# Two layers of a hybrid decoder trunk: the framework's scheduler orders the kernel on another machine model

## Chip, cores and metric

One core of one Trainium2 chip runs the whole kernel. The metric is the device time of one execution in microseconds (us); for the kernel before it is the median of three runs. Engines go by the names of the profile: PE (TensorE matmul), PEld (its weight loads), DVE (VectorE), ACT (ScalarE), POOL (GpSimd), SP (SyncE, which here issues most DMAs).

## The reference, cut to what matters

512 tokens of width 1024 go through two layers. A layer adds three things to x, one after the other: a mixer of three parallel branches, a cross attention over 256 memory tokens, and a gated MLP with a short causal convolution.

```
h = rmsnorm(x)
ya = nsa_attention(...)        # 8 heads: compressed, selected and window attention
yb = hgrn2_recurrence(...)     # gated linear recurrence, 4 heads
yc = gated_deltanet(...)       # delta rule recurrence, 4 heads, triangular solves
merged = sigmoid(h@ma)*(ya@w_branch_a) + sigmoid(h@mb)*(yb@w_branch_b) + sigmoid(h@mc)*(yc@w_branch_c)
x = x + merged @ w_mix_out
x = x + memory_cross_attention(rmsnorm(x), mem_k, mem_v, w_q, q_norm, k_norm, w_o)
x = x + conv_glu_ffn(rmsnorm(x), w_up, conv_w, w_down)     # D_FF = 2816
```

All weights are float32. The three recurrences and attentions of the mixer do not depend on each other; the mixer, the cross attention and the MLP depend on each other in that order, and so do the two layers.

## The kernel before, in words

`tile_trunk` (L200) holds the program. Activations stand as eight tiles of 128 features x 512 tokens. Every dense projection (`dense`, `fm_proj`, `fm_scaled`) goes through `load_w` (L340): SP loads 256 KB of weights into a `wr` buffer (three of them), ACT rounds them to `wh`, DVE subtracts to get the rest `wl` (two buffers of each), and `mm3` issues three matmuls of 128x512 for every 128 rows of weights (high x high, high x low, low x high). One load feeds four times three matmuls. These dense matmuls accumulate in the three `pd` banks. The small matmuls of the recurrences and attentions use two `pa` banks and three `pt` banks; between two of them lie a DVE step, an ACT step, or both.

The order of the program text in a layer is: token projections, delta rule (`gdn`, L518 on: preparation, inverse, levels, a scan over four chunks), HGRN recurrence (`hgrn`, seven levels, then a scan) woven with the preparation of the sparse attention (`nsa_pre`), gates and queries, the attention (`nsa_attn`, 16 steps of one head pair and one block of 128 queries), the three branch projections, the output projection, cross attention (`xattn`, `xo_resid`), MLP (`ffn`). All of this is unrolled.

What sets the order on the engines is not the text but the scheduler of the framework, which works when the `TileContext` closes. Each instruction has a priority from its place in the text. The scheduler plays the program on a machine model: an engine that can take an instruction is given the one of highest priority among those whose inputs and buffers are there in the model's time. The order that results on each engine is written into the program, and the chip runs each engine's list in that order, waiting on semaphores where an input is late. Two kinds of instructions are pulled ahead in priority by 3000 places:

```
with tc.high_priority(PRI):
    act(hi, raw)
    tt(lo, raw, hi.bitcast(F32), SUB)
```

(L345 to L347, the split of the weights) and the scaling that empties a `pd` bank (`fm_scaled`, L446). The numbers of buffers bound how far dense work can run ahead: 16 `gate` tiles hold finished projections, 36 `chain` tiles hold everything of the recurrences and attentions, two `pa` and three `pt` banks hold their products. The helpers `mm` (L236), `act` (L243), `tt` (L246), `ts` (L250, L252) and `stt` (L255) record every operation, so most rows of the profile carry one of these lines.

## Time and profile before

| | us |
|---|---|
| median of 3 runs | 2110.07 |
| lowest, highest | 2108.05, 2112.93 |
| the profiled execution, span from first to last instruction | 2108.7 |
| PE busy in it | 2057.5 |
| DVE busy | 1430.0 |
| ACT busy | 951.3 |
| POOL busy | 131.9 |

The profile lists the span of the profiled execution and no separate time around it; the span lies 1.4 us under the median. Busy time is the time in which at least one instruction of an engine runs. Matmuls overlap each other, so the mean of one is longer than the distance between two.

### The profile page before, as it was taken

The numbers are of one execution on the slowest core, as the hardware profiler recorded it, in microseconds if no ns is written. First come the engines' busy times: TensorE is split into PE (matmuls) and PEld (weight loads), VectorE is DVE, ScalarE is ACT, GpSimd is POOL, SyncE is SP. The second block draws the span as 40 slices with busy tenths as digits, with TensorE's granted clock in tenths as the row PEclk, the third lists the DMA queues.
The fourth block names the chain that finished last, engine by engine and source line by source line (L and its number), as shares of the span: only waits on it lengthen the run. The fifth ranks groups of instructions, "written<-read, shape, count | busy, mean of one in ns | idle before, by whom it ended". The sixth has DMA issues, their size and how long they took to land. (4 is left out here: it accounts for less than half of the span.)

```text
span 2108.7 us, 31046 instructions
## 1 busy us (share of the span) xinstructions
PE 2057.5 (98%) x11396; PEld 1610.2 (76%) x11400; DVE 1430.0 (68%) x3070; ACT 951.3 (45%) x1854; POOL 131.9 (6%) x120
## 2 busy tenths in 40 slices
PE   8999999999999999999999998999999999999999
PEld 7877677777786788888888776777778758888887
DVE  6764898666656887377548469975667577755773
ACT  6434444555545544244434344445554454433442
POOL 1000122000010100000000003110000110000000
PEclk9999999999999999999999999999999999999999
DMA  7332222111241233323432312121113413333333
GB/s 237 90 101 68 77 74 64 52 51 46 64 140 47 88 95 95 95 94 96 120 107 76 101 42 90 59 72 51 46 46 91 126 52 92 95 93 98 95 98 108
DMA packets 116809, 180.90 MB, mean 86 GB/s; under 512 B 19696, under 2 KB 37232, under 8 KB 116656
## 3 DMA queue, kind: packets, MB, share of 16 engines
q1 hardware_dynamic: 88992, 158.64, 25.1%
q10 hardware_dynamic: 27584, 19.97, 3.3%
q8 instruction: 90, 1.47, 0.3%
q14 instruction: 63, 0.52, 0.1%
q0 software_dynamic: 80, 0.29, 0.0%
HBM read 170.21 MB, written 8.65 MB: 85 GB/s over the span
## 5 line engine op out<-in xcount | busy, mean ns | idle before, releaser
L236 PE MATMUL pd<-act,wh 128*128 128x512 f32 x3008 | 985.4, 403 | 0.0
L243 ACT ACTIVATE wh<-wr 128x512 fp32r<-128x512 f32 (+2 forms) x586 | 365.5, 624 | 657.5 <-PE pd L236 566.3
L236 PEld LDWEIGHTS pd<-act,wh 128*128 128x128 f32 x3008 | 560.6, 189 | 128.4 <-issue 14.4
L236 PE MATMUL pd<-act,wl 128*128 128x512 f32 x1504 | 605.6, 403 | 1.4 <-DVE wl L246 1.4
L246 DVE TENSOR_TENSOR wl<-wr,wh 128x512 fp32r<-128x512 f32 (+2 forms) x586 | 406.7, 694 | 212.3 <-ACT wh L243 205.0
L236 PE MATMUL pd<-chain,wh 128*128 128x512 f32 x1344 | 426.7, 397 | 4.4 <-DVE gate L255 3.2
L236 PEld LDWEIGHTS pd<-act,wl 128*128 128x128 f32 x1504 | 284.3, 189 | 69.0 <-issue 6.1
L236 PEld LDWEIGHTS pd<-chain,wh 128*128 128x128 f32 x1344 | 251.0, 188 | 66.0 <-ACT chain L243 3.7
L236 PE MATMUL pd<-chain,wl 128*128 128x512 f32 x672 | 266.4, 396 | 0.3
L246 DVE TENSOR_TENSOR gate<-pd,rb 128x512 f32<-128x512 f32 x168 | 116.0, 691 | 102.8 <-PE pd L236 101.3
L236 PE MATMUL pa<-chain,chain 128*64 128x64 f32 (+7 forms) x1248 | 163.2, 296 | 2.3 <-ACT chain L243 1.0
L236 PEld LDWEIGHTS pd<-chain,wl 128*128 128x128 f32 x672 | 126.6, 188 | 30.3 <-DVE wl L246 1.1
L255 DVE SCALAR_TENSOR_TENSOR gate<-gate,vec,gate 128x511 f32<-128x511 f32 (+1 forms) x176 | 132.1, 751 | 21.5 <-ACT gate L243 18.3
L236 PEld LDWEIGHTS pa<-chain,chain 128*64 128x64 f32 (+3 forms) x1248 | 109.1, 163 | 45.5 <-issue 21.0
L1084 DVE TENSOR_REDUCE tiny<-pa 128x1 f32<-128x128 f32 (+3 forms) x128 | 61.1, 487 | 81.7 <-PE pa L236 81.3
L243 ACT ACTIVATE chain<-pa,tiny,r 128x128 f32<-128x128 f32 (+3 forms) x128 | 78.9, 617 | 60.7 <-DVE tiny L246 56.3
L246 POOL TENSOR_TENSOR chain<-chain,t 128x512 f32<-128x512 f32 x30 | 40.7, 1355 | 1014.7 <-ACT t L243 949.0
L243 ACT ACTIVATE chain<-pt 128x512 f32<-128x512 f32 (+3 forms) x156 | 61.1, 445 | 63.9 <-PE pt L1100 37.2
L243 ACT ACTIVATE gate<-gate,vec 128x512 f32<-128x512 f32 x88 | 63.8, 726 | 27.9 <-DVE gate L246 27.9
L236 PE MATMUL pa<-chain,tok 128*64 128x128 f32 x704 | 62.3, 282 | 0.0
L255 DVE SCALAR_TENSOR_TENSOR t<-t,gate 128x512 f32<-128x512 f32 x88 | 60.5, 688 | 2.0 <-ACT t L243 0.4
L246 POOL TENSOR_TENSOR tg<-tg,chain 128x256 f32<-128x256 f32 (+1 forms) x42 | 45.5, 1089 | 191.1 <-ACT tg L243 78.5
(238 smaller groups left out, 2001.5 us busy)
## 6 DMA issues: line engine op xcount, KB each, us to landing
wr<-in_w_fm SPq DMA_DIRECT2D x184, 256.0 KB, 2.7
wr<-in_w_up SPq DMA_DIRECT2D x176, 256.0 KB, 2.6
wr<-in_w_dn SPq DMA_DIRECT2D x64, 256.0 KB, 2.7
wr<-in_w_mix SPq DMA_DIRECT2D x32, 256.0 KB, 2.7
wr<-in_w_dn SPq DMA_DIRECT2D x32, 192.0 KB, 2.4
wr<-in_w_tk SPq DMA_DIRECT2D x16, 272.0 KB, 2.9
wr<-in_w_kv SPq DMA_DIRECT2D x16, 256.0 KB, 3.8
chain<-in_cmp_w SPq DMA_DIRECT2D x16, 256.0 KB, 4.1
```

What stands on the lines that cost most here:

```text
L236: TE.matmul(out_, lhsT, rhs, start=start, stop=stop, skip_group_check=True)
L243: S.activation(o, i, f, **kw)
L246: (eng or V).tensor_tensor(o, x, y, op)
L255: V.scalar_tensor_tensor(o, x, s, y, op0, op1)
L1084: V.tensor_reduce(nm, ps[:, :W], AX.X, MAX, negate=True)
```

## The change

One argument is added where the context is made:

```
-    with tile.TileContext(nc) as tc:
+    with tile.TileContext(nc, schedule_with_timeline_sim=True) as tc:
         tile_trunk(tc, aps, out)
```

`tile_trunk`, the tiles, the buffers and the priorities are the same. The scheduler plays the same instructions on another machine model of the framework (its timeline machine) and writes down the order that comes out there. An instruction stays on its engine. What can differ is the order on every engine, which buffer of a pool a tile gets, which semaphore waits are needed, and where ACT must load another table of functions.

## Rows read from the trace of the kernel before

**Rows 1.** The page: busy time by engine, and the span in 40 slices.
```profile
PE 2057.5 (98%) x11396; PEld 1610.2 (76%) x11400; DVE 1430.0 (68%) x3070; ACT 951.3 (45%) x1854; POOL 131.9 (6%) x120
PE   8999999999999999999999998999999999999999
```
**Rows 2.** Windows: length; busy us of PE, PEld, DVE, ACT, POOL; PEclk; DMA share; GB/s.
```profile
0.00:52.70 52.70, 43.72 (x263) 37.02 (x264) 34.77 (x67) 33.54 (x63) 10.08 (x20) 1.00 0.79 237
52.70:240.00 187.30, 184.66 (x1388) 145.81 (x1389) 117.24 (x294) 78.26 (x152) 6.36 (x7) 0.99 0.29 82
240.00:370.00 130.00, 118.59 (x753) 91.35 (x752) 122.79 (x271) 57.07 (x104) 33.69 (x29) 1.00 0.25 74
370.00:632.00 262.00, 261.76 (x1500) 198.60 (x1499) 163.82 (x408) 135.99 (x321) 7.75 (x6) 1.00 0.23 70
632.00:690.00 58.00, 54.66 (x246) 35.76 (x245) 36.75 (x157) 29.80 (x70) 0.00 (x0) 0.97 0.18 52
...
740.00:1060.00 320.00, 320.00 (x1384) 260.08 (x1383) 211.65 (x314) 131.26 (x208) 6.50 (x5) 1.00 0.33 100
1060.00:1250.00 190.00, 184.88 (x1400) 150.53 (x1401) 111.75 (x259) 78.24 (x149) 6.42 (x7) 0.99 0.29 80
1250.00:1385.00 135.00, 125.21 (x762) 95.57 (x762) 121.28 (x260) 57.48 (x106) 34.64 (x28) 0.97 0.24 74
1385.00:1590.00 205.00, 204.47 (x1281) 150.97 (x1280) 132.93 (x375) 109.60 (x279) 1.29 (x1) 1.00 0.17 51
...
1690.00:1745.00 55.00, 50.63 (x208) 33.58 (x206) 38.54 (x99) 27.93 (x58) 8.66 (x6) 0.97 0.19 54
1745.00:2108.70 363.70, 359.89 (x1555) 292.11 (x1553) 232.81 (x346) 139.80 (x220) 0.00 (x0) 1.00 0.32 97
```
**Rows 3.** Chain that ended last, in order of time: its last piece.
```profile
1744.01 360.90 PE pd L236 x1559
```
**Rows 4.** Waits of PE: us in total, times, longest.
```profile
PE pa L236 <- DVE chain L246: 11.7, 13, 3.1
...
PE pd L236 <- DVE wl L246: 2.2, 5, 0.9
```
**Rows 5.** PE groups, 1385 to 1590: busy us, mean ns, idle before.
```profile
L236 PE MATMUL pd<-act,wh 128*128 128x512 f32 x249 | 88.4, 417 | 0.0
L236 PE MATMUL pd<-act,wl 128*128 128x512 f32 x124 | 51.8, 418 | 0.2 <-DVE wl L246 0.2
...
L236 PE MATMUL pd<-chain,wh 128*128 128x512 f32 x64 | 21.6, 408 | 0.0
...
L236 PE MATMUL pd<-chain,wl 128*128 128x512 f32 x32 | 12.8, 399 | 0.0
```
**Rows 6.** Timeline of PE, 1500 to 1512: start us, us, instructions merged.
```profile
1501.19 0.40 PE L236 MATMUL pd<-act,wh 128*128 128x512 f32 x1
1501.42 0.51 PE L236 MATMUL pa<-chain,chain 128*128 128x384 f32 x2
1501.78 0.23 PE L236 MATMUL pa<-negb,identb 128*128 128x128 bf16 x1
1501.82 0.48 PE L236 MATMUL pd<-act,wh 128*128 128x512 f32 x1
```
**Rows 7.** ACT table loads: the group over the span.
```profile
L243 ACT ACT_TABLE_LOAD x7 | 9.0, 1283 | 1.3 <-PEq L1439 1.2
```
**Rows 8.** Timeline, 246.5 to 253: start us, us, engine; a wait of PE.
```profile
247.43 1.29 POOL L246 TENSOR_TENSOR tg<-tg,chain 128x512 f32<-128x512 f32 x1 [4.45 <-ACT wh L243]
247.48 1.79 DVE L246 TENSOR_TENSOR gate<-gate,chain 128x512 f32<-128x512 f32 x1
...
249.53 0.68 DVE L246 TENSOR_TENSOR gate<-gate,tg 128x512 f32<-128x512 f32 x1
...
252.71 0.46 PE L236 MATMUL pa<-chain,tg 128*128 128x128 f32 x2 [2.68 <-DVE chain L246]
```
**Rows 9.** The page's groups: the weight split on DVE.
```profile
L246 DVE TENSOR_TENSOR wl<-wr,wh 128x512 fp32r<-128x512 f32 (+2 forms) x586 | 406.7, 694 | 212.3 <-ACT wh L243 205.0
```

## The prediction, made before the changed kernel ran

> **What bounds the kernel now.** I read the page's busy lines first [rows 1]: PE is busy 2057.5 of 2108.7 us, in every slice but the first and one other at nine tenths or more. DVE, the next engine, has 68%. So PE sets the time, and an order can win at most what PE stands idle, 51.2 us, plus what is hidden inside its busy time. The second view is the windows [rows 2], because an average over 2.1 ms says nothing of where the 51 us lie. Subtracting PE's busy time from each length gives three kinds of stage.
>
> Dense alone: 740 to 1060 (320.00 of 320) and 1745 to the end (359.89 of 363.7). The chain of waits ends in one piece of 1559 dense matmuls in 360.90 us [rows 3], 231.5 ns each.
>
> Chains under cover: 52.7 to 240 and 1060 to 1250 (delta rule), 370 to 632 and 1385 to 1590 (attention and branches). PE is idle 2.64, 5.12, 0.24 and 0.53 us there, 8.5 of 844.3 us or 1.0%. It isn't because the chains are short: in 1385 to 1590 the groups on `pd` are 249+124+64+32 = 469 dense matmuls [rows 5], and 469 x 231.5 ns = 108.6 us, over half of the 205. The small steps hide between dense ones.
>
> Chains with little cover: cross attention (632 to 690 and 1690 to 1745: idle 3.34 and 4.37, 6.8% of 113 us) and the HGRN recurrence with the preparation of the sparse attention (240 to 370 and 1250 to 1385: idle 11.41 and 9.79, 8.0% of 265 us). In the latter DVE is busy 122.79 of 130 and 121.28 of 135 us, so it is as close to the bound as PE. The third view, PE's waits, agrees: its first group is a wait on a DVE result, 11.7 us in 13 times [rows 4]. In the timeline PE stands 2.68 us before such a product [rows 8]; as its list is in order, dense matmuls placed behind it stand too.
>
> **The change, part by part.** Nothing is removed or added on PE, DVE, POOL or SP but semaphore waits: 11396 matmuls stay 11396. The sum is therefore one of idle time made and unmade, stage by stage.
>
> *Dense stages, 683.7 us:* 0. A dense matmul waits only for its split weights, and the longest such wait on PE is 0.9 us [rows 4]. Idle there is 3.8 us, at the very end, which no order removes. Downwards the bound is 0; upwards it is the weight stream, a rival below.
>
> *Waits at the head of PE's list, in the scan stages:* the old order put a small product ahead of dense ones when its input wasn't there. An order from another machine may put it later. From below it wins all of 11.41 + 9.79 = 21.2 us; from above it wins nothing, or loses as much again where it guesses the DVE chain worse. DVE is the reason against a large win: it has 7.2 and 13.7 us idle in these two stages, and its work is the same. I take 0, with -21 and +21 as ends.
>
> *Cover of the chains:* this is where I expect the loss. The present order is at 1.0% idle because dense tiles are doled out between small steps, a few matmuls at a time [rows 6]. Dense work is a stock: 16 `gate` tiles, three `pd` banks. If the new machine serves ready dense matmuls in longer runs, because its engines fill up earlier or because its prices for the small steps are longer, the stock is used up ahead of the last small steps, and these run bare. A small step that waits behind a longer run also keeps one of only two `pa` banks longer, which holds back the next score. The wait is then on PE, queued behind it the rest of the attention, and behind that the branch, the output projection and the norm, none of which can start early. Price: the lower end is the scatter that the same text already shows between its two layers, 2.64 against 5.12 us in the delta rule stage [rows 2]; doubling the idle time of all four stages would cost 8.5 us. The upper end is that they all run as badly covered as the cross attention: 6.8% of 844.3 = 57.4, less the 8.5 they have, +48.9 us. Between these lies 28.7. I take +25, just below the middle, since the attention, 467 of the 844 us, has now the least idle time of all and so the most room to hide a worse order.
>
> *Start and cross attention:* the first 52.7 us (idle 9.0) stand under the first transfers, with the DMA engines busy 0.79 of the time [rows 2]; the cross attention waits on its own results. Both 0, with ends of a few us either way.
>
> *Table loads on ACT:* seven of 1283 ns [rows 7]. Another order may put other functions between the four Sigmoids and two Ln of a layer. From below 0; from above one more load for each of these twelve, 15.4 us, on an engine that is busy 951.3 of 2108.7 us [rows 1]. I take 0 and keep 15 for the upper end.
>
> Sum on the profiled span: 2108.7 + 0 + 0 + 25 + 0 + 0 = 2133.7 us. The span lies 1.4 under the median of the runs, so the time forecast is 2135 us, 1.2% more.
>
> **A rule weighed against the trace.** Beside POOL's 1.29 us the DVE product at 247.48 took 1.79 us, where its like at 249.53 took 0.68 [rows 8]. The Trainium skill, "SBUF — State Buffer", section "Summary: rules for kernel authors", says that a DVE operation with two SBUF inputs and a GpSimd operation that reads SBUF do not overlap: the later one stands until the first is done. By that rule (this pair agrees: 1.11 us more, against 1.29) any order that newly lays POOL beside DVE costs up to POOL's own time, and POOL has 33.69 and 34.64 us in the scan stages [rows 2], where DVE has no room for it; some of it is paid already. By that rule alone the worst case is some tens of us more, which would land near 2150; it would not change my sum, only press on its upper half.
>
> **The rivals.**
>
> *The new order fits better: faster.* Place: PE's waits in the scan and delta rule stages, 11.41 + 9.79 + 2.64 + 5.12 = 29.0 us of idle time. Price: if half of it goes and no cover is lost, -15, that is 2095 us; if all of it goes, 2081. For it: thirteen waits on the same kind of DVE result [rows 4] look like one misjudged step, which a better clock of the planner would mend everywhere. Against it: the stages are bound by DVE as well, and a PE at 98% has more to lose than to win. It decides if the attention stages keep their idle time near 1%: then nothing offsets the gain.
>
> *The weight stream slips: much slower.* The splits are pulled ahead by 3000 places, but that counts only when an engine is given its next instruction. If the new machine hands out DVE work earlier, a split stands behind operations like itself, 694 ns each [rows 9]. With two buffers of `wl`, one in five of the 586 splits late by one such operation is 117 x 0.694 = 81 us: 2191 us. Against it: DVE is idle 32% of the time, and PE waits for `wl` only 2.2 us in all now.
>
> *No difference.* The switch has no effect, or it moves work only where PE stays full: 2110 us. For it speaks that the dense and attention stages, 1150.7 of the 2108.7 us, have next to no idle time that an order made. Against it: the mixed stages, where thirteen late products already cost 11.7 us [rows 4].
>
> **How the numbers follow.** Cover lost, 0.45, at 2135, with its own range of 2115 to 2175 (from the lower end of the price, with little else, up to the upper end with the table loads). Weight stream or several causes, 0.10, at 2175 and more. Better fit, 0.35, at 2095, from 2075 to 2105. No difference, 0.10. Within 0.2% (4.2 us, about what a measurement of this kernel tells from no change) I put the last case alone: faster 0.35, same 0.10, slower 0.55. As both signs hold much of the chance, the range for 8 in 10 reaches well into the faster case: from 2082, below which lies a bit over a fifth of that case, to 2190, above which lies most of the weight-stream case.
>
> **What would show it.** Right: the windows of 52.7 to 240 and 370 to 632 and their twins have PE idle 4% or so instead of 1%; in the timeline the attention's last steps have no `pd` matmuls between them, and in its first half the runs of `pd` matmuls are longer than two or three; PE's waits are headed by ACT `chain` or DVE `chain` results from the attention. The dense stages keep 231 ns per matmul. Wrong: the attention stays at 1% idle, and the 11.7 us on DVE `chain` are gone (then the time is under 2100); or the waits are on `wl` (the weight stream); or more than seven table loads stand on ACT's path. Wrong in another way: a changed distance between dense matmuls, which no term here has.

## The result, and the profile after

The kernel after takes 2350.41 us, median of 4 runs (2349.68 to 2351.21); the kernel before took 2109.06 in the same comparison (2106.86 to 2112.93). The ratio is 1.1137, 95% interval 1.1122 to 1.1151: 241 us slower, ten times the loss forecast and outside the range. The profiled span is 2347.8 us, 239.1 more than before.

First the page, against [rows 1]: busy time by engine (us, share of the span, instructions), PE's busy tenths and its granted clock in 40 slices.

```profile
PE 2143.4 (91%) x11394; PEld 1705.8 (73%) x11400; DVE 1433.7 (61%) x3070; ACT 967.7 (41%) x1854; POOL 132.8 (6%) x120
...
PE   7999868997789799999999996799877989999999
...
PEclk9999877997789899999999997889877999999999
```

The work is the same, yet PE's busy time grew by 85.9 us (2057.5 to 2143.4). Its idle time grew from 51.2 to 204.4, by 153.2. The two add up to the 239.1 us. The slices show where: the sixes to eights lie in the two stretches with recurrences and attention, and under them the granted clock falls too. It mixes the two levels of 1.2 and 2.4 GHz; a mean of 0.75 is half of the time at the lower one.

Next the windows, cut at the same landmarks of the first layer in both kernels, so that each line holds the same small steps (their counts agree within seven products): (1) tokens and preparation of the delta rule, (2) its levels and scan, and the start of HGRN, (3) to the first `kcT` product, (4) the attention's first block of queries, (5) its blocks 1 to 3, which are its last 12 steps, (6) branches, output projection and cross attention, (7) MLP and the next norm. Columns as in [rows 2]. Before:

```profile
38.70:167.10 128.40, 125.76 (x755) 105.34 (x756) 88.68 (x236) 51.31 (x96) 4.08 (x4) 0.99 0.40 114
167.10:296.30 129.20, 121.63 (x1077) 92.05 (x1076) 91.49 (x188) 57.97 (x112) 21.09 (x21) 1.00 0.24 71
296.30:365.70 69.40, 65.56 (x409) 50.26 (x399) 63.48 (x150) 30.93 (x59) 14.89 (x11) 1.00 0.21 60
365.70:400.30 34.60, 34.60 (x197) 25.46 (x196) 21.06 (x81) 18.77 (x60) 0.00 (x0) 1.00 0.20 61
400.30:545.10 144.80, 144.80 (x923) 106.37 (x921) 91.87 (x251) 78.56 (x197) 0.00 (x0) 1.00 0.15 46
545.10:706.40 161.30, 156.89 (x722) 118.19 (x721) 106.83 (x264) 80.13 (x155) 16.44 (x12) 0.99 0.30 90
706.40:1071.00 364.60, 364.46 (x1579) 296.04 (x1578) 242.09 (x367) 149.85 (x238) 7.79 (x6) 1.00 0.33 99
```

After:

```profile
45.80:208.10 162.30, 162.01 (x916) 134.27 (x917) 97.25 (x240) 61.36 (x111) 4.53 (x4) 1.00 0.35 104
208.10:364.10 156.00, 122.56 (x1060) 99.08 (x1061) 93.33 (x197) 58.85 (x112) 22.43 (x21) 0.87 0.18 56
364.10:433.50 69.40, 61.66 (x356) 49.07 (x346) 53.03 (x118) 27.51 (x52) 11.06 (x9) 0.83 0.13 40
433.50:529.90 96.40, 94.25 (x444) 73.68 (x445) 56.49 (x145) 37.22 (x90) 2.76 (x2) 0.98 0.27 80
529.90:661.80 131.90, 98.54 (x619) 72.92 (x617) 62.22 (x199) 61.32 (x162) 0.00 (x0) 0.75 0.01 3
661.80:835.40 173.60, 156.89 (x692) 117.48 (x688) 102.91 (x257) 77.89 (x149) 16.79 (x12) 0.93 0.24 78
835.40:1197.00 361.60, 361.60 (x1566) 294.30 (x1567) 239.29 (x366) 151.07 (x237) 7.78 (x6) 1.00 0.33 100
```

The lengths alone mislead: the last 12 steps of the attention got shorter, 144.8 to 131.9 us. What moved is seen by taking the matmuls on `pd` alone (same windows 1, 4 and 5; busy us, then the count):

```profile
45.80:208.10 162.30, 131.94 (x577) 1.00 0.35 104
433.50:529.90 96.40, 84.87 (x334) 0.98 0.27 80
529.90:661.80 131.90, 0.18 (x1) 0.75 0.01 3
```

Before, the same three:

```profile
38.70:167.10 128.40, 91.98 (x413) 0.99 0.40 114
365.70:400.30 34.60, 27.00 (x87) 1.00 0.20 61
400.30:545.10 144.80, 88.42 (x305) 1.00 0.15 46
```

So 304 dense matmuls left the last 12 steps, which now hold one, and went into the stages ahead. A dense matmul still takes 231.5 ns from one to the next; the chain's last piece answers to [rows 3]:

```profile
1988.47 355.59 PE pd L236 x1536
```

With that price taken off (length less dense count x 0.2315), each stage shows what its small steps cost beyond dense work:

| stage of layer 1 | dense before / after | us beyond dense before / after | change |
|---|---|---|---|
| 1 tokens, delta preparation | 413 / 577 | 32.8 / 28.7 | -4.1 |
| 2 delta levels and scan, HGRN start | 260 / 241 | 69.0 / 100.2 | +31.2 |
| 3 to the first `kcT` | 192 / 146 | 25.0 / 35.6 | +10.6 |
| 4 attention, block 0 | 87 / 334 | 14.5 / 19.1 | +4.6 |
| 5 attention, blocks 1 to 3 | 305 / 1 | 74.2 / 131.7 | +57.5 |
| 6 branches to cross attention | 535 / 504 | 37.4 / 56.9 | +19.5 |
| 7 MLP | 1571 / 1560 | 0.9 / 0.5 | -0.4 |

The sum is 118.9 us for this layer, by the windows 75.1 us more idle time and 43.8 us more of PE's busy time; in stage 5 alone 33.4 us of idle time and 24.1 us that the same small steps keep PE busy longer. The start adds 7.1 us (38.7 to 45.8), so that 113.1 of the 239.1 us fall to the second layer, which repeats the pattern: its attention blocks 0 to 2 take 96.2, 37.6 and 45.8 us, those of the first layer 96.4, 37.6 and 45.8.

PE's waits, against [rows 4] (us, times, longest):

```profile
PE pa L236 <- ACT chain L243: 73.7, 72, 2.0
PE pa L236 <- DVE chain L246: 45.2, 18, 14.0
PE pa L236 <- ACT tg L243: 8.8, 10, 2.5
PE pd L236 <- DVE wl L246: 8.5, 14, 1.3
```

The first group, of one or two us at a time, was 1.0 us in 2 times before. It lies mostly in the attention: 24.4 of the 33.4 us that PE stands idle in stage 5 are spent before score products, until ACT's exponential of an earlier score is done, and PE has nothing else to issue. The queries and keys of such a product were made before these steps; by the program, what the exponential gives back is the `pa` bank that it reads, one of two. The timeline of PE in stage 5 shows such a step (start us, us, instructions merged, idle before):

```profile
590.99 1.01 PE L236 MATMUL pa<-chain,chain 128*128 128x384 f32 x2 [1.30 <-ACT chain L243]
591.80 0.33 PE L236 MATMUL pa<-negb,identb 128*128 128x128 bf16 x1
591.92 2.77 PE L1100 MATMUL pt<-cm,chain 128*128 128x128 f32 x12
594.62 2.76 PE L236 MATMUL pa<-chain,tok 128*64 128x128 f32 x24
...
600.05 0.62 PE L236 MATMUL pa<-chain,chain 128*128 128x384 f32 x2 [1.57 <-ACT chain L243]
```

In [rows 6] a dense matmul stood on either side of each small group; here none does. Over PE's whole list the dense matmuls stood in 444 runs of 15.2 on average before, and in 209 runs of 32.4 after. The MLP's long runs make most of these averages; the median run went from 3 to 12, the size of one load.

What longer runs do to the stock is seen at the start of stage 2, in the first 276 small products of the delta rule there (the same in both kernels but for four). Matmuls on `pd`, before and after:

```profile
167.10:190.45 23.35, 11.83 (x38) 1.00 0.26 74
```
```profile
208.10:249.90 41.80, 29.67 (x121) 1.00 0.24 74
```

PE is busy all the time in both, and beyond dense work they take 14.6 and 13.8 us. But before, runs of one to four covered them with 38 dense matmuls; after, runs of 12 to 21 spent 121 on the same cover.

The longest wait, 14.0 us, is a single place of the HGRN levels, and it returns with the same length in layer 2 (up to 1468.65 us):

```profile
321.64 3.76 PE L236 MATMUL pa<-chain,tg 128*128 128x128 f32 x16 [14.02 <-DVE chain L246]
325.05 1.20 PE L236 MATMUL pd<-act,wh 128*128 128x512 f32 x2
```

Dense matmuls follow it at once: they stood behind it in the list. The table loads are 7 as before [rows 7].

### The profile page after: what moved, and what is told of

It is laid out like the page before. It is cut to its first block, busy times and chain, and to the rows that moved or that the text cites. A ratio compares the mean times of both kernels' runs of the same rounds, so it can differ in the third digit from the quotient of the medians.

```text
span 2347.8 us, 31062 instructions
## 1 busy us (share of the span) xinstructions
PE 2143.4 (91%) x11394; PEld 1705.8 (73%) x11400; DVE 1433.7 (61%) x3070; ACT 967.7 (41%) x1854; POOL 132.8 (6%) x120
## 4 chain that ended last, share of the span: by engine, by line
PE 82%; DVE 11%; ACT 4%; issue 2%; DMA 1%; ACTq 0%; DVEq 0%
PE pd L236 65%; PE pa L236 13%; PE pt L1100 3%; ACT chain L243 2%; DVE chain L246 2%; DVE tiny L1084 1%; DVE tg L246 1%; DVE gate L246 1%; DVE chain L865 1%; DVE wl L246 1%; PE pt L236 1%; PE pt L430 1%; DVE tiny L246 1%; DVE chain L250 0%; ACT tg L243 0%
## 5 line engine op out<-in xcount | busy, mean ns | idle before, releaser
L236 PE MATMUL pd<-act,wh 128*128 128x512 f32 x3008 | 957.5, 399 | 6.6 <-DVE gate L246 6.6
L236 PE MATMUL pa<-chain,chain 128*64 128x64 f32 (+7 forms) x1248 | 187.0, 322 | 67.7 <-ACT chain L243 64.2
L236 PEld LDWEIGHTS pa<-chain,chain 128*64 128x64 f32 (+3 forms) x1248 | 117.4, 177 | 109.8 <-ACT chain L243 83.2
L236 PEld LDWEIGHTS pd<-chain,wl 128*128 128x128 f32 x672 | 127.4, 190 | 32.8 <-DVE wl L246 3.3
L255 DVE SCALAR_TENSOR_TENSOR gate<-gate,vec,gate 128x510 f32<-128x510 f32 (+1 forms) x176 | 131.7, 750 | 18.4 <-ACT gate L243 15.5
L236 PE MATMUL pa<-chain,tg 128*128 128x128 f32 (+2 forms) x352 | 56.9, 332 | 47.1 <-DVE chain L246 42.7
L243 ACT ACTIVATE chain<-pt 128x512 f32<-128x512 f32 (+3 forms) x156 | 66.3, 443 | 74.4 <-PE pt L1100 54.7
L236 PEld LDWEIGHTS pa<-chain,tg 128*128 128x128 f32 (+2 forms) x352 | 47.8, 223 | 53.9 <-POOL chain L246 28.5
L1100 PE MATMUL pt<-cm,chain 128*128 128x128 f32 x320 | 69.7, 389 | 6.4 <-DVE chain L250 5.4
```

What stands on the lines that cost most here:

```text
L236: TE.matmul(out_, lhsT, rhs, start=start, stop=stop, skip_group_check=True)
L243: S.activation(o, i, f, **kw)
L255: V.scalar_tensor_tensor(o, x, s, y, op0, op1)
L1100: TE.transpose(pst[:, k * P:(k + 1) * P], pr[:, k * P:(k + 1) * P], ident)
```

## The experiments

The theory (called A in the expectations) is the prediction's likeliest case: the timeline machine serves ready dense matmuls in long runs, so the chains run bare. In the labels df is the order of the default machine (the kernel before), tl that of the timeline machine (the kernel after). Medians are given with their ratio to the kernel before, run on the same chip.

**1. df_first: dense work first, on the default machine.**

```
 def mm3(ps, w, k, act_, start, stop):
+    with tc.high_priority(6000):
         ... the three matmuls
```

> The default machine, with the dense matmuls raised by 6000 places over everything else, so that a dense matmul that is ready always goes first and the small steps of the chains wait. Theory A (the loss of the changed kernel is the order on PE alone: dense work is used up early, the chains run bare afterwards): this kernel has no dense matmul left between the attention's steps at all, so it should be as slow as the changed kernel or slower, 2350 to 2450 us, with PE idle over 8% of the span and a granted clock under 0.95. Rival B (the loss comes from something else that the other machine changes: buffers, waits, the lists of DVE, ACT and the DMA queues): the default machine keeps its own way with these, and the time stays under 2200 us.

Measured: 2522.03 us, 1.1943 [1.1918, 1.1967]. The page of that kernel:

```profile
PE 2214.5 (88%) x11400; PEld 1752.1 (70%) x11400; DVE 1439.6 (57%) x3070; ACT 968.8 (38%) x1854; POOL 127.7 (5%) x120
...
PE   8997767797779899999999958687977898999999
```

Served dense first, the machine of before makes a kernel with the same pattern of slices, with dense runs of 80.6 on average and none in blocks 1 to 3. The direction is as A has it; the size is above what was expected. A cover used up early can cost 400 us, so the 241 need no other mechanism; that there is no other, this run doesn't show.

**2. tl_load2 and df_load2: loads of half the size.** Runs of whole loads become runs of half.

```
-for k0 in range(0, n, 4):
-    kn = min(4, n - k0)
+for k0 in range(0, n, 2):
+    kn = min(2, n - k0)
```

> The timeline machine, with every dense weight load halved (two blocks of 128 rows, six matmuls, instead of four blocks and twelve). Theory A1 (this machine gives PE every matmul the moment its inputs are there, and a small step that comes a little later stands behind all of them; so what counts is how many dense matmuls become ready at once): the runs of dense matmuls get shorter, the stock lasts longer, and the loss against the default machine on the same halved loads falls by a third or more, from 241 us to under 165. Rival A2 (the machine's prices for the small steps put the dense work early, whatever its grain): the loss stays at 220 to 260 us.

> The control to the halved loads: the default machine with loads of six matmuls. Twice as many loads, splits and DMAs, each shorter. Both theories: PE's work is the same, DVE and ACT have some 60 us more of fixed costs, so 2110 to 2150 us.

Measured: tl_load2 2336.19 us, 1.1074 [1.1051, 1.1097]; df_load2 2135.85, 1.0114 [1.0091, 1.0137]. The loss between the two machines falls from 241 to 200 us, between what the two versions of the theory expected, and decides for neither.

**3. tl_held and tl_fine: dense work held back for the attention.** Eight gate projections a layer (24 dense matmuls each) are tied into eight of the last 12 steps. In tl_held a whole projection may go behind the step's first score product; in tl_fine each three matmuls wait for another of eight small products of the step.

```
+for s_, _ in enumerate(nsa_attn(l, tok, ya, st)):
+    if s_ in HOLD:
+        with tc.issue_after(st["anchor"]):     # tl_held
+            gate(*queue.pop(0))
...
+        with tc.issue_after(behind.pop(0)):    # tl_fine, around each mm3
```

> The timeline machine, with eight gate projections per layer (192 dense matmuls, 44 us of PE) tied behind the first score matmul of eight of the attention's last twelve steps, on PE's list only. In the changed kernel these eight stand in the attention's first quarter. Theory A (the stock is used up early): the first quarter gets some 44 us shorter, the last three grow by much less, as the held matmuls fall into PE's idle time and keep the clock up; 25 to 45 us less per layer, 2260 to 2300 us in all, and the granted clock in the attention rises over 0.95. Rival B (the chains are slow for another reason): the held matmuls come on top, the attention as a whole stays at 228 us per layer, and the time stays at 2340 to 2360 us.

> The timeline machine, with the same eight gate projections held in the attention as in the run that held them whole, but cut up: of the 24 matmuls of a projection each three stand behind another small product of the step (four scores, four transposes). Theory D (the loss is the grain: a small step stands behind one or two whole weight loads, 12 to 24 matmuls or 2.8 to 5.6 us, and then its own DVE and ACT steps pass with PE idle, so dense and chain run one after the other): three matmuls, 0.7 us, fit beside a DVE or ACT step, the held matmuls cost next to nothing, and the attention gets 25 to 40 us shorter per layer than with the whole runs, 2389 down to 2310 to 2340 us. Theory A as first put (only the stock counts): no difference to the run that held them whole, 2380 to 2395 us.

Measured: tl_held 2388.82 us, 1.1316 [1.1295, 1.1338]; tl_fine 2350.05, 1.1139 [1.1116, 1.1161]. The same block (i = 2, four steps) of the kernels before, after, tl_held and tl_fine:

```profile
442.10:491.50 49.40, 49.40 (x312) 36.11 (x311) 31.00 (x85) 25.41 (x65) 0.00 (x0) 1.00 0.14 44
```
```profile
567.50:613.30 45.80, 33.56 (x206) 24.77 (x206) 20.80 (x69) 20.12 (x54) 0.00 (x0) 0.74 0.00 1
```
```profile
513.20:575.50 62.30, 51.52 (x278) 39.37 (x278) 26.75 (x78) 25.25 (x63) 0.00 (x0) 0.77 0.08 26
```
```profile
507.40:558.10 50.70, 44.84 (x279) 32.13 (x279) 27.38 (x78) 25.95 (x63) 0.00 (x0) 0.94 0.10 32
```

Both times lie outside what either theory expected, tl_held's above and tl_fine's between. Theory A as first put, that it is enough to keep a stock, falls: with 72 dense matmuls in the block, tl_held takes 62.3 us where the bare block takes 45.8, so 16.5 of the 16.7 us (72 x 0.2315) came on top. Spread in threes, the same matmuls take 50.7 us: 4.9 more than bare, and 11.6 less than in tl_held, of which 4.9 are idle time (10.8 to 5.9) and 6.7 PE's busy time (51.5 to 44.8). So in these steps it takes a fine grain to hide dense work; a stock alone doesn't. The gain of 39 us over tl_held left tl_fine no faster than the kernel after: the cover held back for these steps was missing ahead of them, where block 0 now has no dense matmul and takes 39.6 us, against 19.1 us beyond dense work in the kernel after. The loss is a balance over the whole layer, and this local repair doesn't pay.

**4. tl_last and df_last: is it priority?** As df_first, with `tc.high_priority(-6000)`: all dense work last wherever something else is ready.

> The timeline machine, with the dense matmuls lowered by 6000 places. Theory D (this machine puts a matmul in PE's line as soon as its inputs are there, so that a small step that comes later finds the line full, whatever its priority): 2340 to 2360 us, as the changed kernel. Rival P (the loss comes of priorities, of the weight splits pulled ahead by 3000 places above all): small steps go first again, most of the loss goes, under 2200 us.

> The default machine, with the dense matmuls lowered by 6000 places, so that any small step that is ready goes first. On this machine priority decides between what is ready when PE is free (raising them by as much cost 19%), so the order should change, but small steps are rarely kept waiting there already: 2095 to 2125 us.

Measured: tl_last 2349.54 us, 1.114 [1.1112, 1.1168]; df_last 2135.21, 1.0124 [1.01, 1.0149]. On the default machine the priority of the dense matmuls decides: 6000 places up cost 411 us (experiment 1), 6000 down 26. On the timeline machine 6000 places down moved the time by 0.9 us, which is D's case of the expectation, and PE's list is the one of the kernel after in 11310 of 11400 places (by tiles and shapes in the traces). Its rival P falls for the matmuls' own priority; the 3000 places of the weight splits were not touched. df_last was expected a little faster than before and is 1.2% slower.

**5. tl_load1 and df_load1: loads of one block.** A load feeds only three matmuls, so no more than three become ready at once.

```
+for k0 in range(0, n):
+    kn = 1
```

> The timeline machine, with every dense weight load cut to one block of 128 rows, three matmuls. Halving the loads took the loss against the default machine from 241 to 200 us. Theory D (grain): three matmuls at a time can hide beside the chains' DVE and ACT steps, so the loss against the default machine on the same loads falls well under half, to 40 to 120 us. Rival A2 (the machine's prices put dense work early whatever its grain, and the step from 241 to 200 was a side effect): 170 us or more.

> The control: the default machine with loads of three matmuls. Four times as many loads and splits; halving them cost 1.1%. Two halvings, the second with twice as many new operations: 2160 to 2250 us, and DVE and ACT over 75% and 55% busy.

Measured: tl_load1 2611.15 us, 1.2373 [1.2355, 1.2392]; df_load1 2634.77, 1.248 [1.2462, 1.2499]. The difference of the machines is gone, even turned by 24 us, but both lie outside their expectations (df_load1 was put at 2160 to 2250), because another bound has come. Waits of PE in df_load1:

```profile
PE pd L236 <- ACT wh L243: 170.0, 450, 2.2
PE pd L236 <- DVE wl L246: 47.9, 80, 2.1
```

PE waits for the split of its weights everywhere, so the pair is no clean control of grain. It agrees with A inside the attention: blocks 1 and 2 of tl_load1 hold 143 and 160 dense matmuls and take 21.2 and 25.4 us beyond them; in the kernel before, with 95 and 105, they take 19.7 and 25.2.

**6. tl_warm, tl_pd2 and tl_warm2: what is the lower clock worth?** tl_warm adds four products of 384 columns a step to the last 12 steps, into an unused part of a `pa` bank. tl_pd2 is a control with two `pd` banks, the third written once (the cross attention's third accumulator moves to a `pt` bank); tl_warm2 adds to it 96 products of 512 columns a layer, one behind each small group of the last 12 steps. No result of the added products is used.

```
+if i:                                   # tl_warm, in each step
+    for pr in prs:
+        mm(po[:, P:], pr[:, :P], cm[:, :T - P])
...
+for ins in st["anchor"] if s_ > 3 else ():   # tl_warm2
+    with tc.issue_after(ins):
+        mm(warm, identb, negt)
```

> The timeline machine, with four more matmuls of 384 columns in each of the attention's last twelve steps of a layer (96 in all, their products are not used), placed where PE waits for the copies of the transposed probabilities. They add 96 x 0.32 us = 31 us of PE work at the high clock. Theory C (much of the loss is the clock that falls in the bare steps): the half clock goes from these steps and they get shorter in spite of the added work, by 5 to 15 us per layer, 2320 to 2340 us. Theory D (the chain's DVE and ACT steps set the pace there, the clock adds little): no gain, 2350 to 2390 us, even if the granted clock rises.

> The control to the next run: the timeline machine with two pd banks instead of three; the freed bank takes the product of one matmul that nothing reads. The dense stages have one bank less to run ahead in: 2350 to 2390 us, with the attention's last twelve steps bare as in the changed kernel.

> As the control with two pd banks, and 96 bf16 matmuls of 512 columns per layer, whose products are not used, each tied on PE's list behind one of the small products of the attention's last twelve steps; they read constants, and write the free bank only, so no small step waits for a buffer because of them. They add 20 to 30 us of PE per layer, where PE is idle or slow. Theory C (a good part of the loss in the bare steps is the lower clock): the half clock goes and these steps get shorter, 5 to 20 us per layer less than the control. Theory D alone (DVE and ACT set the pace there): the steps stay within 3 us of the control or get longer by the matmuls that stand in the way, up to 25 us per layer.

Measured: tl_warm 2451.8 us, 1.1624 [1.1606, 1.1643], its mean clock 0.928 (after: 0.932). The run is slower than either theory expected. The trace has 192 more matmuls, two for each added product, so the added work was twice the 31 us counted on; PE is busy 2211.7 us, and the clock stayed where it was. A new wait heads the list, 61.5 us in 24 times on DVE's scaled probabilities; that it comes of a `pa` bank kept longer by the added products was not tested. tl_pd2 2335.16, 1.1064 [1.1046, 1.1082]: a bank less made this order 15 us faster, against what was expected. tl_warm2 2358.43, 1.1172 [1.1155, 1.1189]. Block i = 2 in tl_pd2, then in tl_warm2:

```profile
564.20:607.40 43.20, 31.62 (x207) 23.82 (x207) 21.05 (x69) 20.87 (x54) 0.00 (x0) 0.81 0.00 1
```
```profile
569.10:612.70 43.60, 33.27 (x235) 21.74 (x239) 21.21 (x69) 20.62 (x54) 0.00 (x0) 0.96 0.00 1
```

The clock rose from 0.81 to 0.96 and the block did not get shorter; the other two blocks got 5 to 6 us longer (their clocks went from 0.91 to 0.89 and from 0.82 to 0.87). That is the case put down for D. But what the higher clock gave back and what 32 more matmuls cost (207 weight loads became 239; 28 of the matmuls were recorded) can't be parted here. The clock's own share of the loss stays open; if it shows only in PE's busy time, it is at most the 86 us by which that grew.

**7. tl_dflist and df_tllist: PE's list exchanged.** The program is first scheduled by one machine and the order of PE's instructions kept; then it is scheduled by the other, with each PE instruction tied behind its predecessor in that list. Only PE's list is given; DVE, ACT, POOL and the queues are ordered, around it, by the machine named first in the label.

```
+for first, then in zip(like or (), (like or ())[1:]):
+    tc.add_manual_dep(pe[then], first, mybir.DependencyInfo(
+        mybir.DependencyClass.NoSync, mybir.DependencyReason.DATA), reason="PE list")
...
+_, pe_list = traced()                                       # default machine
+nc, _ = traced(pe_list, schedule_with_timeline_sim=True)    # tl_dflist
```

> The timeline machine orders everything, but PE's instructions are tied, one behind the other, in the order that the default machine gives them; DVE, ACT, POOL and SP keep what the timeline machine makes of that. Theory L (PE's list alone carries the loss): within 1.5% of the kernel before, 2080 to 2145 us. Rival B (the other engines' lists, buffers and waits carry half or more): 2230 us or more.

> The reverse: the default machine orders everything, with PE's instructions tied in the order of the timeline machine's list. Theory L: as slow as the changed kernel, 2310 to 2380 us, with the granted clock under 0.95 and PE idle over 180 us. Rival B: under 2230 us.

Measured: tl_dflist 2144.23 us, 1.0166 [1.0151, 1.0181]; df_tllist 2361.96, 1.1199 [1.1181, 1.1218]. Page of tl_dflist, then its first wait of PE:

```profile
PE 2062.8 (96%) x11400; PEld 1618.4 (76%) x11400; DVE 1423.7 (67%) x3070; ACT 957.3 (45%) x1854; POOL 131.2 (6%) x120
```
```profile
PE pd L236 <- DVE wl L246: 28.3, 22, 4.6
```

The same of df_tllist, with two waits:

```profile
PE 2129.8 (90%) x11400; PEld 1694.4 (72%) x11400; DVE 1440.8 (61%) x3070; ACT 962.2 (41%) x1854; POOL 129.1 (5%) x120
```
```profile
PE pa L236 <- ACT chain L243: 73.5, 75, 1.8
PE pa L236 <- DVE chain L246: 49.3, 16, 10.7
```

This settles the main cause. PE's lists came out as meant: by tiles and shapes in the traces, tl_dflist has the list of the kernel before in all 11400 places, df_tllist that of the kernel after in all but two. With PE's list of before, the timeline machine's kernel loses 1.7%, just inside L's 2080 to 2145 us; with PE's list of after, the default machine's kernel loses as much as the kernel after, with the same two waits at the head. So 206 of the 241 us (85%) go and come with the order of PE's instructions. It isn't PE's list quite alone, because the machine plans the other engines around it: a DVE instruction of tl_dflist stands 2.7 places on average from its place in the kernel before and 23.6 from that in the kernel after. A list of DVE or ACT that doesn't fit PE's was not run. PE's busy time follows the list as well: 2062.8 and 2129.8, against 2057.5 and 2143.4. The remaining 34 us are what the timeline machine's other choices (lists of the other engines, buffers, waits) cost with this PE list, and there the first wait is on late `wl` splits, 28.3 us where [rows 4] had 2.2. The two parts needn't add up: in the other direction PE's list alone costs 252 us, more than the whole loss.

## Why the prediction was wrong

**What bounds the kernel: right as far as it went.** PE set the time and its order was what moved. That an order can win at most 51.2 us of idle time, plus what hides in the busy time, says nothing of what it can lose.

**Dense stages, 0: right.** 231.5 ns a matmul, and the MLP stage moved by 0.4 us.

**Cover of the chains, +25 and at most +48.9: the step that failed.** The mechanism is the one forecast, and its signs came: runs longer (median 3 to 12), no `pd` matmul in the last steps, waits headed by ACT `chain` and DVE `chain`. Its size was wrong: the attention alone lost 62.1 us in the first layer (stages 4 and 5) and about as much in the second, where the term had 25 for all covered stages of both. The runs show two reasons. First, the ceiling was read off the cross attention, with PE idle 6.8% of the time. Bare attention steps have 25% (33.4 of 131.9 us): between two of its products lie ACT and DVE steps, and only the cover had hidden them. The cross attention of the kernel before wasn't bare either: in the kernel after PE is idle 10.0 of the 40 us from 770 to 810. The kernel before never ran these steps bare, so no row of it had this share; the number of small steps and their ACT and DVE times would have been the row to build a ceiling from. Second, the sum counted idle time only. PE's busy time grew by 86 us, a third of the loss: the transposes of the attention (L1100) took 279 ns on average before and 389 after, at a granted clock of 0.75 in their stretch. The last line of "what would show it" had named only a changed pace of dense matmuls, which stayed.

A third point completes the mechanism. The text put the loss on a stock used up early, and the start of stage 2 shows that, 121 dense matmuls where 38 had covered the same products. But tl_held kept a stock for the attention and lost more: in these steps the cover has to stand between the small products, a few matmuls at a time; whole projections came on top of the chain.

**Scan stages, 0 with ends of -21 and +21 over both layers: wrong.** Stages 2 and 3, which hold them and the delta levels, lost 31.2 and 10.6 us in the first layer. The prediction had allowed for a worse guess of the DVE chain, but only for as much again as PE was idle there; one place now waits 14.0 us in either layer, with dense matmuls behind it. Of the 25.9 us more idle time in stage 2 another 11.0 lie in 250 to 302 us, where the products of the delta rule's scan stand with little dense work, and belong to the lost cover. PE's busy time in stages 2 and 3 hardly changed (121.6 and 65.6 to 122.6 and 61.7), with 19 and 46 dense matmuls fewer and a granted clock of 0.87 and 0.83.

**Start and cross attention, 0: wrong for the second.** Stage 6, which has the branches too, lost 19.5 us: 12.3 us more idle time, most of it in the cross attention (10.0 us in 770 to 810), and the same PE busy time with 31 dense matmuls (7.2 us) fewer. The start's 7.1 us lie near the few us that were kept as its ends.

**Table loads, 0: right.** Seven, as before.

**The rule on POOL and DVE.** A pair side by side is dear in the kernel after too (a `gate` product at 306.00 took 1.51 us beside POOL's 1.27), but busy time of DVE and POOL grew by 3.7 and 0.9 us only [rows 1]. As far as busy time tells, the new order laid hardly more of them together than the old one. The tens of us that the prediction worked out by the Trainium skill's rule in "SBUF — State Buffer" (section "Summary: rules for kernel authors") did not come.

**The rivals.** "Better fit" fell: PE's waits on DVE `chain` went from 11.7 to 45.2 us. "No difference" fell. "The weight stream slips" was right in its place and minor in its size: 8.5 us of waits on `wl` in the kernel after, and 28.3 in tl_dflist, where PE is otherwise full. With 0.45 on the right mechanism, the range still missed, because its upper end was a ceiling that a well-covered kernel can't show.

**What stays open.** Why the timeline machine hands out dense matmuls in longer runs wasn't tested; the runs show that it does, and that a lower priority of theirs doesn't change it. The clock's share of the 86 us wasn't parted from that of fewer overlaps between neighbours. What a third `pa` bank would save in the bare steps, whose score products wait for one, wasn't tested either.

## What to carry to other kernels

An engine at 98% says how little a new order can win, not how much it can lose: the ceiling of the loss is what the small steps cost bare, which their own ACT and DVE times can bound (not tried here), not the idle share of another stage. When the order of a full engine changes, count dense work per stage and the length of its runs before looking at waits; a stage may get shorter in the windows and still have lost most. Dense work hides a chain when it lies between the chain's products in small pieces: what a piece spends beyond the wait that it covers is missing later.

## What had not been expected of the hardware

PE's busy time is no constant of the work: with the same matmuls it was 2057.5, 2143.4 and 2214.5 us (before, after, df_first), rising as the granted clock of the span fell, 0.995, 0.932, 0.896. The clock isn't all of it: in df_load1, whose loads feed three matmuls each, it was 2350.7 us at a clock of 0.991.

Of the seven windows the one with the lowest clock, 0.75, is the one where PE stood idle for a quarter of the time, in gaps of at most two us; in 302 to 326 us, around the wait of 14.0, it was 0.57. In tl_fine the steps of block i = 2 with 72 dense matmuls in threes ran at 0.94, and with them in whole projections at 0.77. The Trainium skill, "TensorE: Matmul & The Clock Gate", section "Part 1: The HAM clock gate", has the clock set by how busy the PE has been recently. These stretches agree with it in direction, but the busy share of a stretch alone doesn't tell its clock: 0.77 with PE busy 83% of the block in tl_held, 0.96 with 76% in tl_warm2. A cover that is lost can so show up a second time, in the matmuls that are left.
